# Pacing the sample's steps against the prompt's: four entries of a table

## The chip, the cores and the metric

The kernel runs on one core of a Trainium2 chip. The metric is the device time of one execution in microseconds (us). Runs before the change gave a median of 1927.56 us (three runs, 1924.34 to 1928.93).

## The reference, cut to what matters

One layer of a decoder is computed for two groups that share the weights: a prompt of 1024 tokens, and a sample of 8 sequences with one new token each and 8192 cached positions. All is float32.

```python
# prompt
q, k, v, logf, u, z = mixer_inputs(rmsnorm(xp, g_mix), w_in, b_f, g_sgu_v)
xp = xp + merge_heads(fox_prompt(q, k, v, logf), sgu_prompt(u, z, w_s, b_s), g_att_out, g_sgu_out, w_o)
xp = xp + cross_attend(rmsnorm(xp, g_cross), *memory_kv(mem_prompt, g_mem, w_ck, w_cv), w_cq, w_co)
xp = xp + conv_ffn(rmsnorm(xp, g_ffn), zeros, w_up, conv_w, conv_b, w_down)[0]
# sample: the same layers; the attention reads the paged cache through page_table
att = fox_sample(q, k, v, logf, cache_k, cache_v, cache_logf, page_table)   # 8 rows x 8192 positions x 8 heads x 64
xs = xs + merge_heads(att, sgu_sample(u, z, w_s, b_s), ...)                # w_o
xs = xs + cross_attend(rmsnorm(xs, g_cross), cache_mem_k, cache_mem_v, w_cq, w_co)
xs = xs + conv_ffn(rmsnorm(xs, g_ffn), state_conv, w_up, conv_w, conv_b, w_down)[0]
```

## The kernel before, in words

**The prompt** is one Python generator (`prompt`). Its float32 products are each made as three TensorE products of split operands (`gemm3`, L246 to L248; in the projection L410 to L412): ScalarE rounds a loaded weight tile `wr` to `wh` (L209), VectorE takes the rest `wl` (L210). The stages, by the names that the table `PACE` uses: `p1` the input projection; `att0` and `att1` the attention of each half of the tokens; then for each half `mid0`/`mid1` (output projection `w_o`, cross-attention with `w_cq` and `w_co`) and `ffn0`/`ffn1` (the MLP: 22 pairs of `w_up` tiles in four groups, each group followed by its `w_down` part). In `out_proj` the residual is added on VectorE (L932), the row factor of the norm goes through ScalarE (L948) and GpSimd (`fac`, L949) to a ScalarE scaling (L955), and `norm_T` turns the rows on TensorE (L992) and splits them on ScalarE and VectorE (L212, L213). The stretch from the last residuals of `w_co` to those splits is called the junction below; there are four of them, before `w_cq` and before `w_up` in each half.

**The sample** is a second generator. `decode` has 148 steps. A step of it loads 1 MB of keys through a GpSimd indirect DMA (L1287), multiplies them with the query on VectorE (L1293) and sums (L1297): 128 K steps, 16 for each of the 8 rows. A value step follows 18 steps later: 1 MB of values (L1346) and four column-tiled matmuls (L1352), issued for two steps at a time. Between them stand the softmax pieces of each row (L1309 to L1341). After it `sample_rest` has 87 steps: `w_o`, `w_cq`, the cross-attention's keys (`cmk`, L1516 and L1517 on VectorE, then transposes on TensorE, L1522) and values (`cmv`, L1549), `w_co` (L258), and the MLP, which reads all of `w_up` (L1591, L1595, L1610) and `w_down` (L1629, L1634) once more, 1 MB a load, and ends in two small sums (L1647) that take a PSUM bank from the ring of the prompt's products. All of the sample's large loads share four buffers of 1 MB, `kv`, and go through GpSimd's queue.

**The pace.** The prompt's generator yields after each portion of work an estimate of its TensorE time; the driver adds it up and issues one step of the sample whenever the sum reaches the entry of `PACE` for the stage. Once `decode` is through, `phase[1]` is `"rest"`, and that entry holds until the end. A flag (`held`) lets no step be issued while a junction before an MLP or a cross-attention is issued. The numbers are units of the estimate, of which the prompt has 1483 in all; they are not microseconds of the trace.

```python
        acc[0] += t
        most = int(t / PACE[phase[1] or phase[0]]) + 1
        while bgs and not held[0] and most and acc[0] >= PACE[phase[1] or phase[0]]:
            most -= 1
            acc[0] -= PACE[phase[1] or phase[0]]
            if next(bgs[0], None) is None:
                bgs.pop()
```

The tile layer then orders the issued instructions engine by engine, and hands out the buffers of a ring in the order of issue: a prompt tile that was issued behind a sample tile of the same ring gets no bank before that one has been served. On each engine instructions then run in the written order.

Of the kernel before, what the change touches and what calls it, by code (L numbers as in the profile page):

```python
# [72 lines left out]
KS = 2  # L73
BKQ = 1
LA = (2, 2)
PACE = {'p1': 7.5, 'att0': 20.0, 'mid0': 8.0, 'ffn0': 9.0, 'att1': 15.0, 'mid1': 7.5, 'ffn1': 2.5, 'rest': 3.3}


def build(nc, tc, ctx, a, phases=None):
# [1664 lines left out]
    for t in prompt():  # L1744
# [6 lines left out]
# [6 lines that stand above are left out]
# [94 lines left out]
```

## Time and profile before

| | |
|---|---|
| median of 3 runs | 1927.56 us (1924.34 to 1928.93) |
| profiled execution: its time, its span | 1927.71 us, 1926.0 us |
| granted TensorE clock, mean | 0.971 |
| TensorE matmul busy | 1821.5 us (95%) |
| TensorE weight loads busy | 1305.7 us (68%) |
| VectorE busy | 1403.7 us (73%) |
| ScalarE busy | 761.3 us (40%) |
| GpSimd busy | 470.1 us (24%) |
| DMA | 517.07 MB, mean 268 GB/s |

Busy shares are averages over stages with different limits. In this execution the projection runs to about 340 us, the two attention stages mostly lie between 340 and 520 us, the first half's middle between 520 and 740 us, the first MLP between 740 and 1160 us, the second half's middle to 1400 us, and the second MLP from there to the end. Busy TensorE time counts matmuls as the profile models them, and says where TensorE waits, not how near it is to its peak.

### The profile page before, as it was taken

How to read it: one execution, taken by the hardware profiler on the slowest of the kernel's cores; microseconds unless marked ns; L12 is line 12 of the kernel's file. 1: busy time of each engine (PE TensorE's matmuls, PEld its weight loads, DVE VectorE, ACT ScalarE, POOL GpSimd, SP SyncE). 2: the span in 40 equal slices, each digit the busy share in tenths (PEclk: the TensorE clock that was granted, in tenths of full speed). 3: DMA queues.
4: the chain of work that ended last, by engine and by line, in shares of the span. 5: the costliest groups of instructions: out<-in, count | busy, mean ns of one | idle time of the engine just before them, and what ended most of it. 6: DMA issues, size and time to landing. Idle time of an engine off the chain costs nothing.

```text
span 1926.0 us, 24250 instructions
## 1 busy us (share of the span) xinstructions
PE 1821.5 (95%) x9255; PEld 1305.7 (68%) x9255; DVE 1403.7 (73%) x1662; ACT 761.3 (40%) x1435; POOL 470.1 (24%) x429
## 2 busy tenths in 40 slices
PE   8999989788899899999999999998999999999986
PEld 5987667555676667777777776765776576876752
DVE  4887668777687776999899999878777255965412
ACT  5332366566632435323333333325344143243311
POOL 1322241222122322324123124133312201210121
PEclk9999999889999999999999999999999999999978
DMA  8876897644496865869677889877767945857785
GB/s 321 292 267 224 294 347 263 226 144 160 159 366 256 321 232 211 333 245 367 256 280 298 297 313 362 327 295 276 277 242 255 355 171 206 293 218 217 257 315 199
DMA packets 156372, 517.07 MB, mean 268 GB/s; under 512 B 20168, under 2 KB 41928, under 8 KB 123488
## 3 DMA queue, kind: packets, MB, share of 16 engines
q0 software_dynamic: 56400, 339.04, 47.0%
q1 hardware_dynamic: 92944, 163.89, 24.2%
q10 hardware_dynamic: 6912, 12.59, 1.7%
q8 instruction: 73, 1.20, 0.2%
q14 instruction: 43, 0.35, 0.1%
HBM read 493.63 MB, written 21.84 MB: 268 GB/s over the span
## 4 chain that ended last, share of the span: by engine, by line
PE 64%; DVE 6%; issue 6%; ACT 3%; POOL 1%; DMA 1%; POOLq 0%; DVEq 0%; ACTq 0%
PE ba L246 11%; PE ba L247 11%; PE ba L248 11%; PE bb L246 5%; PE dv L1352 5%; PE bb L247 5%; PE bb L248 5%; DVE kv L1293 1%; DVE s L1297 1%; PE ba L1078 1%; PE bb L772 1%; PE ba L728 1%; PE bb L756 1%; PE ba L1104 1%; DMA kv<-w_down 1%
## 5 line engine op out<-in xcount | busy, mean ns | idle before, releaser
L209 ACT ACTIVATE wh<-wr 128x1024 fp32r<-128x1024 f32 (+2 forms) x220 | 229.0, 1044 | 457.5 <-PE ba L247 145.9
L210 DVE TENSOR_TENSOR wl<-wr,wh 128x1024 fp32r<-128x1024 f32 (+2 forms) x220 | 261.7, 1201 | 114.7 <-PE ba L248 50.2
L1293 DVE TENSOR_TENSOR kv<-kv,d 128x2048 f32<-128x2048 f32 (+1 forms) x139 | 292.3, 2114 | 35.8 <-DMA kv<-cache_k,kidx 35.7
L1297 DVE TENSOR_REDUCE s<-kv 128x32 f32<-128x2048 f32 (+1 forms) x139 | 292.1, 2108 | 0.8
L1287 POOL DMA_INDIRECT kv<-cache_k,kidx x128 | 172.1, 1345 | 493.6 <-DVE s L1297 191.0
L1346 POOL DMA_INDIRECT kv<-cache_v,kidx x128 | 171.0, 1336 | 487.8 <-DVE s L1297 216.1
L246 PE MATMUL ba<-wh,u 128*128 128x512 f32 (+1 forms) x679 | 261.0, 386 | 0.1
L247 PE MATMUL ba<-wl,u 128*128 128x512 f32 (+1 forms) x679 | 258.5, 382 | 0.0
L248 PE MATMUL ba<-wh,u 128*128 128x512 f32 (+1 forms) x679 | 256.1, 381 | 0.0
L246 PE MATMUL ba<-u,wh 128*128 128x512 f32 (+2 forms) x552 | 216.5, 393 | 1.5 <-DVE u L213 1.1
L247 PE MATMUL ba<-u,wh 128*128 128x512 f32 (+2 forms) x552 | 216.3, 392 | 0.3 <-DVE u L213 0.3
L248 PE MATMUL ba<-u,wl 128*128 128x512 f32 (+2 forms) x552 | 215.1, 390 | 0.0
L246 PEld LDWEIGHTS ba<-wh,u 128*128 128x128 f32 x679 | 128.1, 189 | 36.4 <-issue 10.5
L247 PEld LDWEIGHTS ba<-wl,u 128*128 128x128 f32 x679 | 128.2, 189 | 31.6 <-issue 7.6
L248 PEld LDWEIGHTS ba<-wh,u 128*128 128x128 f32 x679 | 127.9, 188 | 31.3 <-issue 6.5
L1352 PE MATMUL dv<-kv,s 128*32 128x512 f32 x1024 | 134.0, 611 | 0.0
L246 PEld LDWEIGHTS ba<-u,wh 128*128 128x128 f32 x552 | 104.9, 190 | 36.6 <-issue 10.1
L246 PE MATMUL bb<-u,wh 128*128 128x512 f32 (+2 forms) x312 | 124.2, 398 | 1.7 <-DVE u L213 1.7
L247 PEld LDWEIGHTS ba<-u,wh 128*128 128x128 f32 x552 | 105.1, 190 | 29.4 <-issue 7.2
L247 PE MATMUL bb<-u,wh 128*128 128x512 f32 (+2 forms) x312 | 123.4, 396 | 0.0
L248 PEld LDWEIGHTS ba<-u,wl 128*128 128x128 f32 x552 | 104.9, 190 | 26.6 <-issue 4.6
L248 PE MATMUL bb<-u,wl 128*128 128x512 f32 (+2 forms) x312 | 122.4, 392 | 0.0
(404 smaller groups left out, 2969.1 us busy)
## 6 DMA issues: line engine op xcount, KB each, us to landing
wr<-w_up SPq DMA_DIRECT2D x88, 512.0 KB
kv<-w_up POOLq DMA_DIRECT2D x22, 1024.0 KB
wr<-w_down SPq DMA_DIRECT2D x40, 512.0 KB
kv<-w_down POOLq DMA_DIRECT2D x11, 1024.0 KB
wr<-w_in SPq DMA_DIRECT2D x16, 512.0 KB
wr<-w_o SPq DMA_DIRECT2D x16, 512.0 KB
wr<-w_cq SPq DMA_DIRECT2D x16, 512.0 KB
wr<-w_co SPq DMA_DIRECT2D x16, 512.0 KB
```

Source lines behind the costliest of these rows:

```text
L209: nc.scalar.activation(h, src, AF.Copy)
L210: nc.vector.tensor_tensor(l, src, h.bitcast(F32), op=ALU.subtract)
L246: mmul(out, sh, mh, start=(i == 0), stop=False)
L247: mmul(out, sh, ml, start=False, stop=False)
L248: mmul(out, sl, mh, start=False, stop=(i == n - 1))
L728: mmul(s, qab[j][:, 0, i * P : (i + 1) * P], ka[j][:, ch * n : ch * n + n], start=True, stop=False)
L756: nc.tensor.transpose(tr[:, c * P : (c + 1) * P], p_[:, kt * P : (kt + 1) * P], ident)
L1287: nc.gpsimd.indirect_dma_start(kv, None, a["cache_k"], off(kidx[:, b, ch : ch + 1]))
L1293: nc.vector.tensor_tensor(kvv[:, i : i + m, :], kvv[:, i : i + m, :], qb.unsqueeze(1).broadcast_to((P, m, 512)), op=ALU.mult)
L1297: nc.vector.tensor_reduce(s[:, ch * 4 + i : ch * 4 + i + m, :].rearrange("p k h -> p (k h)"), kvv[:, i : i + m, :].rearrange("p k (h d) -> ...
L1346: nc.gpsimd.indirect_dma_start(kv, None, a["cache_v"], off(kidx[:, b, ch : ch + 1]))
L1352: mmul(dv[32 * j : 32 * j + 32, :], s[:, ch * 4 : ch * 4 + 4, :].rearrange("p k h -> p (k h)"), kvv[:, j, :], start=(ch == 0), stop=(ch == ...
```

## The change

Four entries of the table are smaller, so a step of the sample is issued after less of the prompt's work in the projection (7.5 to 7.0), the first MLP (9.0 to 8.5), the second half's middle (7.5 to 6.8) and in everything that follows `decode` (3.3 to 2.9). No instruction is added or removed; their places change.

```diff
-PACE = {'p1': 7.5, 'att0': 20.0, 'mid0': 8.0, 'ffn0': 9.0, 'att1': 15.0, 'mid1': 7.5, 'ffn1': 2.5, 'rest': 3.3}
+PACE = {'p1': 7.0, 'att0': 20.0, 'mid0': 8.0, 'ffn0': 8.5, 'att1': 15.0, 'mid1': 6.8, 'ffn1': 2.5, 'rest': 2.9}
```

Counted in the order in which the two kernels are issued, the steps of `decode` lie like this:

| stage | p1 | att0 | att1 | mid0 | ffn0 | mid1 | ffn1 |
|---|---|---|---|---|---|---|---|
| before | 28 | 6 | 5 | 21 | 41 | 23 | 25 |
| after | 30 | 6 | 5 | 21 | 44 | 24 | 19 |

The 149th of these calls already enters `sample_rest`, whose further 87 steps follow in `ffn1` in both.

## The prediction

> **What bounds the kernel now.** I read the engines' busy time first, then their course in 40 slices, then tables of busy time by stage, then the time lines of the places that stand out. The slices show an attention part in which no engine is full, a long part in which TensorE is, and a fall at the end:
>
> ```profile
> PE 1821.5 (95%) x9255; PEld 1305.7 (68%) x9255; DVE 1403.7 (73%) x1662; ACT 761.3 (40%) x1435; POOL 470.1 (24%) x429
> PE   8999989788899899999999999998999999999986
> DVE  4887668777687776999899999878777255965412
> ```
>
> The stages (window; busy us and count of TensorE, its weight loads, VectorE, ScalarE, GpSimd; granted clock; DMA share; GB/s) are the projection without its start, the first MLP, two junctions of the second half, the start of the second MLP, the sample's cross-attention keys, and three pieces of the end:
>
> ```profile
> 60.00:340.00 280.00, 273.85 (x1507) 212.08 (x1494) 218.53 (x210) 116.46 (x205) 75.94 (x59) 0.99 0.78 279
> 790.00:1155.00 365.00, 365.00 (x1692) 269.33 (x1691) 339.15 (x315) 123.30 (x190) 103.69 (x73) 1.00 0.80 296
> 1225.00:1262.00 37.00, 33.77 (x175) 26.20 (x174) 30.30 (x33) 12.14 (x24) 6.80 (x7) 0.95 0.62 228
> 1380.00:1402.00 22.00, 17.46 (x91) 12.71 (x90) 21.20 (x16) 13.55 (x25) 10.16 (x9) 0.96 0.74 283
> 1410.00:1550.00 140.00, 140.00 (x694) 92.64 (x694) 82.66 (x107) 45.54 (x71) 28.85 (x28) 1.00 0.75 282
> 1627.00:1690.00 63.00, 63.00 (x273) 51.12 (x272) 60.70 (x58) 18.25 (x26) 13.85 (x23) 1.00 0.79 278
> 1797.00:1848.00 51.00, 51.00 (x400) 35.71 (x392) 15.23 (x22) 13.57 (x26) 9.30 (x13) 1.00 0.77 272
> 1848.00:1904.00 56.00, 41.31 (x262) 16.72 (x258) 2.12 (x5) 4.02 (x8) 11.42 (x16) 0.76 0.86 322
> 1904.00:1926.00 22.00, 12.51 (x49) 8.66 (x49) 11.19 (x22) 5.93 (x16) 3.71 (x5) 0.84 0.25 98
> ```
>
> In both MLPs TensorE is never without work, so there the time is TensorE's work, the prompt's and the sample's. The change alters no work: it can only alter the time that TensorE stands idle. So each edit is costed at the place it leaves and the place it enters, by TensorE's idle time there.
>
> **Prices.** A prompt product takes 0.23 us of TensorE, a pair of value steps 1.85 us, so 0.93 us a step. A K step takes VectorE 2.28 + 2.28 = 4.56 us (medians in the first MLP):
>
> ```profile
> 1362.34 1.85 PE dv L1352 x16
> 1364.62 0.23 PE ba L247
> L1293 DVE TENSOR_TENSOR kv<-kv,d x35: 2269/2281/2335, 796.6 to 1144.9; 128x2048 f32<-128x2048 f32 x35
> L1297 DVE TENSOR_REDUCE s<-kv x37: 2262/2277/2293, 789.1 to 1147.8; 128x32 f32<-128x2048 f32 x37
> ```
>
> **The change part by part.** The steps are unchanged in number; 2 of them move into the projection, 3 into the first MLP, 1 into the second half's middle, 6 out of the second MLP. Of those 6 calls 4 had a K step before, none has one after; the last K step is issued before the junction into the second MLP.
>
> *The last junction (1380 to 1402 us).* Here VectorE's queue holds six halves of K steps among the residuals that TensorE's transposes wait for. The time line of VectorE, and GpSimd's row factors (in brackets the idle time before one, and what ended it):
>
> ```profile
> 1379.84 2.28 DVE L1293 TENSOR_TENSOR kv<-kv,d 128x2048 f32<-128x2048 f32 x1
> 1382.15 2.29 DVE L1297 TENSOR_REDUCE s<-kv 128x32 f32<-128x2048 f32 x1
> 1384.36 0.68 DVE L932 TENSOR_TENSOR u<-ba,u 128x512 f32<-128x512 f32 x1
> 1384.95 2.28 DVE L1293 TENSOR_TENSOR kv<-kv,d 128x2048 f32<-128x2048 f32 x1
> 1387.27 2.29 DVE L1297 TENSOR_REDUCE s<-kv 128x32 f32<-128x2048 f32 x1
> 1389.47 0.68 DVE L932 TENSOR_TENSOR u<-ba,u 128x512 f32<-128x512 f32 x1
> 1393.20 2.28 DVE L1293 TENSOR_TENSOR kv<-kv,d 128x2048 f32<-128x2048 f32 x1
> ...
> 1398.27 2.27 DVE L1297 TENSOR_REDUCE s<-kv 128x32 f32<-128x2048 f32 x1
> 1381.09 1.44 POOL L949 TENSOR_TENSOR fac<-fac,mhalf 128x1 f32<-128x1 f32 x1 [10.13 <-ACT fac L948]
> 1393.86 2.04 POOL L949 TENSOR_TENSOR fac<-fac,mhalf 128x1 f32<-128x1 f32 x1 [2.81 <-ACT fac L948]
> 1400.98 0.54 POOL L949 TENSOR_TENSOR fac<-fac,mhalf 128x1 f32<-128x1 f32 x1 [5.08 <-ACT fac L948]
> ```
>
> The changed order has no K step in this stretch; in its place stand the softmax pieces of the last row, most of them a fraction of a microsecond, two of them sums of about 1.1 us. TensorE is idle for 22.0 - 17.46 = 4.5 us here. I take 4.0 of them as gained; the bounds are 0 (the softmax pieces delay as much) and 4.5.
> The factor's 1.44 and 2.04 us against 0.54 us fall where a K product is running: both end 0.4 us after that product does (1382.12 and 1395.48). The Trainium skill, "SBUF — State Buffer", section "SBUF: two separate sides", says that a VectorE instruction with two SBUF inputs and a GpSimd one that reads SBUF exclude each other through a shared port. The trace agrees with it; by that rule (2.04 - 0.54 = 1.5 us of the idle time is this lock) the gain lies at the upper bound and the sum would be 0.5 us lower.
>
> *The junction before the second half's cross-attention (1225 to 1262 us).* K halves between its last residuals and splits: 9 before, 7 after. Idle 37.0 - 33.77 = 3.2 us; 2/9 of it is 0.7 us. Bounds 0 and 3.2.
>
> *Value steps.* Six leave the second MLP, where TensorE has no idle time: 6 x 0.93 = -5.6 us. Three enter the first MLP, equally full: +2.8 us. Three enter the projection (whose end, with the start of the attention, leaves 280.0 - 273.85 = 6.2 us idle) and the second half's middle; idle time covers them, at +2.8 us if it does not, and I take +0.5. Together -2.3 us, bounds -2.8 and 0.
>
> *The projection's K steps.* Two more, 9.1 us of VectorE, which is idle for 280.0 - 218.53 = 61 us there. What can show is a load that arrives late with VectorE's queue behind it: the prompt's splits and evacuations, for whose PSUM banks TensorE waits. The waits by releaser of this window have three such, 14.3 us, the longest 4.8:
>
> ```profile
> DVE kv L1293 <- DMA kv<-cache_k,kidx: 14.3, 3, 4.8
> ```
>
> One more wait of that kind is the upper bound, 4.8; less than nothing would need a wait that goes, for which no reason is seen. TensorE lost 6.2 us in all beside these 14.3, so I take +0.5.
>
> *The first MLP's K steps.* Three more: 13.7 us of VectorE. Its idle time is 365.0 - 339.15 = 25.9 us, so I cost them at nothing; the cover is this idle time, and without it they cost 13.7 us (a rival below).
>
> *The sample's later layers.* In the order of TensorE the sample's transposes of the keys' scores (L1522) come 248 prompt products after its `w_cq` ends, where they came 284 after it: 36 x 0.23 = 8.3 us earlier. They need the last of eight sums on VectorE, which ends at 1683.71 + 2.28 = 1686.0 us:
>
> ```profile
> 1683.71 2.28 DVE L1517 TENSOR_REDUCE sS<-kv 128x8 f32<-128x2048 f32 x1
> L1522 PE MATMUL ms<-cp,sS x2: 271/272/272, 1692.6 to 1692.7; 128*32 128x128 f32 x2
> ```
>
> The margin was 1692.6 - 1686.0 = 6.6 us, and VectorE was busy for 60.70 of 63 us. In the new order more of the prompt's VectorE work stands among these sums (35 instructions, 24.9 us by their times here, for 24 with 21.0). If VectorE is late by all that, TensorE waits 8.3 + 3.9 - 6.6 = 5.6 us, and all prompt products queue behind L1522. Against it: VectorE's newest prompt work ahead of the last sum is further behind TensorE in the new order, so it starts with less to do. I take +0.5, bounds 0 and 5.6.
>
> *The tail.* One would expect most here: from 1848 to 1904 us TensorE executes nothing of the prompt, because the sample's last sums hold a place in the ring of PSUM banks and the prompt's next tile waits behind them. The denser pace moves that place, but does not free it: in the new order the same block (the last four of eleven pairs of `w_up`, all of `w_down`) stands before product 5449 of 5760 instead of 5716, and the pairs ahead of it come 22 products apart as before. So 312 products follow the block instead of 45, and the block stays as long: 56 us, of which 56.0 - 41.31 = 14.7 us are idle even by the profile's generous count. I cost this at 0. Bounds: -14.7 us, if the sample's loads get ahead; and +6.5 us, since the prompt now has loads left that can compete with the sample's: four buffers of 512 KB, 2.1 MB at the 322 GB/s of this window:
>
> ```profile
> wr<-w_up SPq DMA_DIRECT2D x88, 512.0 KB
> ```
>
> **The sum**: -4.0 - 0.7 - 2.3 + 0.5 + 0 + 0.5 + 0 = -6.0 us. The profiled execution took 1927.71 us, 0.15 above the median of the three runs, so the forecast is 1921.7 us, 0.3% below. About 0.2%, 3.9 us, is what a measurement can tell from no change.
>
> **The rivals.**
> *VectorE becomes the bound of the first MLP.* It is busy for 339.15 of 365 us there, and no row shows whether a queue that runs in order can use the last 7%. If none of its idle time can be used, the 13.7 us come on top: 1921.7 + 13.7 = 1935.4 us, slower. It decides once VectorE's work between two K steps exceeds TensorE's: 339.15 + 13.7 = 352.9 against 365 + 2.8, so 15 us of idle time have to be out of reach. For it speaks how full the queue is; against it that TensorE shows no idle time there at all. [...] Chance 0.27.
> *The cross-attention's wait.* L1522 comes too early by the full 5.6 us in place of 0.5: 1921.7 + 5.1 = 1926.8 us, no change. For it speaks a VectorE at 96%, against it the newest work behind TensorE. Chance 0.15.
> *The tail closes.* The block's idle time goes, the sample being further on when the prompt meets it: 1921.7 - 14.7 = 1907.0 us. Against it speaks the order, which has the same pairs left. Chance 0.08. That the denser pace does nothing at the end is thus my forecast itself.
>
> **How the numbers follow.** The forecast's case has 0.50. Its own range, with the junctions' and the small terms' bounds, is 1917 to 1926 us; 0.40 of it lies more than 0.2% below the median, 0.10 within it. The cross-attention's wait gives 0.10 within and 0.05 above 0.2%. So: faster 0.40 + 0.08 = 0.48; the same 0.10 + 0.10 = 0.20; slower 0.05 + 0.27 = 0.32. The range of 8 in 10 takes in the forecast, the wait, and the first MLP's rival up to 1937 us; downward it reaches to 1912 us, some way into a partly closed tail, and leaves out the rest of that.
>
> **What would show it.** Right: at the junction into the second MLP no L1293 among the residuals, `fac` at about 0.55 us, and TensorE idle for about 0.5 us. The block without prompt products lies at least 61 us earlier (267 products by 0.23 us), is about 56 us long, and full-speed products 0.23 us apart follow it for over 70 us. The first MLP is about 3 us longer, with no TensorE waits. Wrong: waits of TensorE or its weight loads for VectorE in the first MLP (the first rival); idle time ahead of L1522 (the second); a block well under 50 us (the third), or one over 62 us, which I would have mis-sized.

## The result and the profile after

The changed kernel takes 1940.41 us (median of 6 runs, 1934.43 to 1943.31), the kernel before 1926.69 us (median of 6, 1917.97 to 1932.44): the ratio is 1.0071, 95% interval 1.0049 to 1.0093. It is 0.7% slower where 0.3% faster was forecast, and lies above the whole range. The profiled execution took 1940.05 us with a span of 1938.3 us, 12.3 us more than the span before.

The busy time of the changed kernel and its course in 40 slices:

```profile
PE 1820.7 (94%) x9255; PEld 1299.1 (67%) x9255; DVE 1405.0 (72%) x1662; ACT 759.4 (39%) x1435; POOL 488.2 (25%) x429
PE   8999989778899999999999999997999998999798
DVE  4888668777687777989898988887754459553144
PEclk9999999889999999999999999998999998999899
```

TensorE does the same work in the same busy time (1820.7 us for 1821.5). The 12.3 us are idle time of TensorE: 102.5 us between its first and last matmul, where it was 88.3. The hole at the end of the slices has moved forward, from the 40th slice to the 38th; a dip in the 28th is deeper than before, and a small one in the 34th is new.

To find the place, each stretch is bounded by two of the prompt's 5760 products (single TensorE matmuls of its split operands, in their order), so that it holds the same prompt work in every kernel. Lengths in us, worked out from the TensorE rows; three experiments, told of below, stand beside the two kernels. Each column is one execution: that of the last took 1917.65 us, where the median of its kernel is 1912.9.

| prompt products | before | only "rest" denser | only the first three denser | after | after, last sums out of the ring |
|---|---|---|---|---|---|
| start to 2064 (to the first MLP) | 781.5 | 780.5 | 778.6 | 776.6 | 779.8 |
| 2064 to 3504 (first MLP) | 379.1 | 379.0 | 383.4 | 383.5 | 383.7 |
| 3504 to 3888 | 118.2 | 118.2 | 116.1 | 118.7 | 116.0 |
| 3888 to 3984 (second cross-attention) | 72.3 | 77.7 | 82.9 | 85.2 | 83.0 |
| 3984 to 4080 | 24.3 | 24.3 | 26.2 | 26.1 | 26.1 |
| 4080 to 4176 (last junction) | 33.5 | 32.4 | 29.3 | 30.6 | 30.7 |
| 4176 to 4656 | 139.5 | 139.5 | 139.9 | 139.9 | 139.9 |
| 4656 to 5040 (most of the second group's `w_up` part, its `w_down` part) | 103.4 | 103.4 | 111.9 | 111.4 | 112.8 |
| 5040 to 5715 (with the block) | 254.4 | 274.5 | 228.4 | 247.9 | 226.1 |
| 5715 to the end | 19.8 | 18.3 | 17.8 | 18.4 | 17.8 |
| span | 1926.0 | 1947.8 | 1914.5 | 1938.3 | 1915.9 |

Against before, the changed kernel loses 12.9 us in the second cross-attention, 8.0 in the stretch at 4656 and 4.4 in the first MLP, and gains 4.9 us ahead of the first MLP, 2.9 in the last junction and 6.5 in the stretch of the block. Windows of the changed kernel (busy us and count of TensorE, its weight loads, VectorE, ScalarE, GpSimd; granted clock; DMA share; GB/s) over the first MLP, the second cross-attention, the last junction, the middle of the stretch at 4656, and the block:

```profile
776.60:1160.10 383.50, 382.84 (x1766) 276.25 (x1764) 353.37 (x326) 128.94 (x197) 125.49 (x78) 1.00 0.80 296
1278.80:1364.00 85.20, 71.82 (x328) 44.83 (x327) 67.24 (x62) 34.93 (x79) 29.99 (x22) 0.92 0.84 318
1390.10:1420.70 30.60, 28.76 (x143) 22.34 (x141) 18.66 (x26) 18.21 (x33) 6.34 (x7) 0.94 0.69 254
1622.30:1643.80 21.50, 13.63 (x49) 10.53 (x49) 21.50 (x25) 4.66 (x7) 1.99 (x3) 0.76 0.67 224
1802.30:1856.90 54.60, 39.52 (x261) 14.91 (x259) 5.60 (x10) 6.94 (x13) 11.42 (x16) 0.84 0.87 339
```

The kernel before in the second cross-attention and the last junction:

```profile
1278.80:1351.10 72.30, 66.93 (x313) 42.49 (x312) 58.86 (x60) 33.90 (x78) 25.57 (x18) 1.00 0.80 305
1375.40:1408.90 33.50, 28.96 (x139) 23.30 (x138) 25.06 (x23) 17.15 (x32) 10.86 (x9) 0.90 0.74 283
```

So TensorE's idle time goes from 5.4 to 13.4 us in the cross-attention and from 4.5 to 1.8 in the junction; in the block it is 15.1 us, as before.

**The cross-attention.** What TensorE waits for there in the changed kernel (us in total, times, longest), and the piece of the chain of waits that leads to the longest of these (start, length):

```profile
PE ba L1062 <- DMA t<-o_mk: 6.7, 1, 6.7
PE ba L1096 <- ACT u L1089: 6.1, 2, 3.3
```

```profile
1299.55 0.37 SPq L223
1299.97 16.21 DMA t<-o_mk
1316.32 1.10 PE ba L1062 x4
```

The 256 KB of the prompt's memory keys take 16.2 us to land, in a stretch in which the core's DMA moves 318 GB/s, most of it the sample's gathered keys and values (GpSimd's queue moves 15.25 of the 18.52 MB from 1285 to 1345 us). Before, the same load was issued at 1298.5 us and had landed at 1305.7, 7.2 us later, and TensorE had other work until then. The waits of the kernel before, for the scaled weights of ScalarE (L1096) and for the keys of the next head:

```profile
PE ba L1096 <- ACT u L1089: 2.6, 2, 1.9
PE bb L1062 <- DMA t<-o_mk: 0.5, 1, 0.5
```

So two waits have grown: that for the keys to 6.7 us, and that for ScalarE from 2.6 to 6.1.

**The stretch at 4656.** Here TensorE has one long wait, and VectorE's queue shows why. First the wait, then TensorE around it, then VectorE during it (start, length; in brackets the idle time):

```profile
PE bb L246 <- DVE t L1178: 7.9, 1, 7.9
```

```profile
1626.28 0.40 PE L248 MATMUL ba<-wh,u 128*128 128x512 f32 x1
1634.55 0.76 PE L246 MATMUL bb<-wh,u 128*128 128x512 f32 x1 [7.87 <-DVE t L1178]
1635.11 0.63 PE L247 MATMUL bb<-wl,u 128*128 128x512 f32 x1
...
1638.95 0.61 PE L247 MATMUL ba<-wl,u 128*128 128x512 f32 x1
1639.38 0.42 PE L246 MATMUL ba<-wh,u 128*128 128x512 f32 x1
1639.63 0.39 PE L247 MATMUL ba<-wl,u 128*128 128x512 f32 x1
```

The order in VectorE's queue is seen best in the chain of waits, which runs through VectorE alone in these microseconds (the piece called issue is a weight split on VectorE, L210, 1.21 us long):

```profile
1625.22 2.27 DVE kv L1516 x2
1627.48 2.17 DVE sS L1517
1629.66 1.07 issue
1630.73 1.22 DVE kv L1516
1631.95 0.66 DVE t L1175
1632.61 1.13 DVE kv L1516
1633.74 0.66 DVE t L1176
1634.55 0.76 PE bb L246
```

VectorE is busy for all of the 21.5 us (the window above). The products and sums of the sample's cross-attention keys (L1516, L1517) stand between the convolutions of the last `w_up` tiles (L1175, L1176), and the group's `w_down` part, which begins at 1622.3 us, waits 7.9 us for a convolution to free a PSUM bank. It is not the transposes L1522, where the prediction looked for a wait: they start at 1653.7 us without one. Before, this `w_down` part began at 1615.3 us, ahead of the first key product, and VectorE had room:

```profile
1612.00:1660.00 48.00, 48.00 (x210) 35.92 (x210) 35.76 (x35) 10.85 (x14) 12.42 (x21) 1.00 0.74 267
```

### The profile page after: what moved, and what is told of

Same layout as the page of the kernel before. It is cut to its first block, busy times and chain, and to the rows that moved or that the text cites. A ratio compares the mean times of both kernels' runs of the same rounds, so it can differ in the third digit from the quotient of the medians.

```text
span 1938.3 us, 24236 instructions
## 1 busy us (share of the span) xinstructions
PE 1820.7 (94%) x9255; PEld 1299.1 (67%) x9255; DVE 1405.0 (72%) x1662; ACT 759.4 (39%) x1435; POOL 488.2 (25%) x429
## 4 chain that ended last, share of the span: by engine, by line
PE 50%; issue 11%; DVE 7%; DMA 6%; ACT 3%; POOL 3%; POOLq 0%; DVEq 0%; SPq 0%; ACTq 0%
PE ba L246 8%; PE ba L247 8%; PE ba L248 8%; PE bb L246 4%; PE bb L247 4%; PE bb L248 4%; PE dv L1352 4%; DMA kv<-cache_v,kidx 2%; POOL kv L1346 1%; DVE s L1297 1%; DVE kv L1293 1%; PE ba L1104 1%; PE bb L772 1%; DMA t<-o_mk 1%; DMA kv<-w_down 1%
## 5 line engine op out<-in xcount | busy, mean ns | idle before, releaser
L209 ACT ACTIVATE wh<-wr 128x1024 fp32r<-128x1024 f32 (+2 forms) x220 | 228.9, 1044 | 431.7 <-PE ba L247 149.5
L210 DVE TENSOR_TENSOR wl<-wr,wh 128x1024 fp32r<-128x1024 f32 (+2 forms) x220 | 262.1, 1200 | 148.5 <-PE ba L248 71.1
L1287 POOL DMA_INDIRECT kv<-cache_k,kidx x128 | 176.1, 1376 | 570.2 <-DVE s L1297 250.3
L1346 POOL DMA_INDIRECT kv<-cache_v,kidx x128 | 190.2, 1486 | 374.3 <-DVE s L1297 151.7
L246 PE MATMUL ba<-u,wh 128*128 128x512 f32 (+2 forms) x560 | 218.9, 392 | 1.1 <-DVE u L213 0.7
L247 PE MATMUL ba<-u,wh 128*128 128x512 f32 (+2 forms) x560 | 219.3, 392 | 0.1
L1352 PE MATMUL dv<-kv,s 128*32 128x512 f32 x1024 | 134.1, 609 | 0.0
L246 PE MATMUL bb<-wh,u 128*128 128x512 f32 (+1 forms) x313 | 122.1, 390 | 8.7 <-DVE t L1178 7.9
L248 PEld LDWEIGHTS ba<-u,wl 128*128 128x128 f32 x560 | 105.8, 189 | 34.3 <-issue 12.6
L246 PE MATMUL bb<-u,wh 128*128 128x512 f32 (+2 forms) x304 | 121.3, 399 | 2.2 <-DVE u L213 2.2
L247 PE MATMUL bb<-u,wh 128*128 128x512 f32 (+2 forms) x304 | 120.9, 398 | 0.0
```

The source lines that it names most:

```text
L209: nc.scalar.activation(h, src, AF.Copy)
L210: nc.vector.tensor_tensor(l, src, h.bitcast(F32), op=ALU.subtract)
L246: mmul(out, sh, mh, start=(i == 0), stop=False)
L247: mmul(out, sh, ml, start=False, stop=False)
L248: mmul(out, sl, mh, start=False, stop=(i == n - 1))
L1287: nc.gpsimd.indirect_dma_start(kv, None, a["cache_k"], off(kidx[:, b, ch : ch + 1]))
```

## The experiments

**Each half of the change.** The first kernel keeps the three paces of `decode` and makes only `rest` denser, the second does the reverse.

```diff
-'p1': 7.5, 'ffn0': 9.0, 'mid1': 7.5, 'rest': 3.3
+'p1': 7.5, 'ffn0': 9.0, 'mid1': 7.5, 'rest': 2.9     # only rest
+'p1': 7.0, 'ffn0': 8.5, 'mid1': 6.8, 'rest': 3.3     # only the first three
```

> Only the sample's later layers are denser (3.3 to 2.9); the decode's steps stand as in the kernel before. In the order of TensorE everything up to the sample's key transposes (L1522, before product 5217 of the prompt) is as before, so the profile should match the kernel before up to about 1690 us. Theory A (the loss of the changed kernel comes from where the decode's steps, and with them the sample's cross-attention, now fall): no wait of 8 us in the second half's cross-attention and none among the sample's keys; the time differs from before only by the tail, within 4 us of it. Rival B (the denser later layers are the loss, through VectorE among the sample's keys): 8 to 9 us slower than before. Rival C (the first MLP's VectorE): no change.

> The three decode entries are changed, the later layers keep 3.3. The order is that of the changed kernel up to L1522 (before product 4981 in both). Theory A: both waits are there as in the changed kernel, 13 us idle against 5 in the second half's cross-attention and about 9 us among the sample's keys, 3 us less at the junction into the second MLP; the time is 10 to 15 us over before. Rival B: the wait among the keys is gone, at most 5 us over before.

Measured: only `rest` 1948.42 us against 1925.55, ratio 1.0109 (1.0083 to 1.0134); only the first three 1918.90 us, ratio 0.9961 (0.9944 to 0.9979). One half of the change makes the kernel faster and the other, by more, slower: -6.6 and +22.9 us, together +16.3, where both at once measure +13.7. Both expectations missed the time, since both took the tail for unchanged: within 4 us of before was expected of the first, and 10 to 15 us over before of the second, whose two waits did come (10.7 and 9.9 us of idle time). By the table, the first three bring the loss of 19 us in the two stretches with them, but also a gain of 26.0 us between 5040 and 5715, and `rest` costs 20.1 us in that same stretch. In the order of instructions, `rest` alone changes nothing on any engine before the sample's own MLP. The block without prompt products, in the kernel with only `rest`; the whole tail from 5424 to 5715 in that with only the first three:

```profile
1788.00:1887.00 99.00, 77.28 (x547) 37.19 (x545) 6.61 (x13) 10.07 (x18) 21.25 (x30) 0.69 0.87 324
```

```profile
1789.90:1896.70 106.80, 101.89 (x595) 67.83 (x592) 40.45 (x64) 32.06 (x60) 13.40 (x19) 1.00 0.64 229
```

Between two neighbouring prompt products the longest gap is 57.9 us before, 98.7 with only `rest`, 17.7 with only the first three, 54.6 with all four. The place of the sample's last sums in the ring of PSUM banks is set by the pace at which the steps are issued: 87 steps by 0.4 puts it 35 units of the estimate earlier when `rest` is denser. But how far the sample is at that place isn't set by this pace: its pairs of `w_up` come 22 products apart from product 5314 on with both values of `rest` (before, with the old paces of `decode`, from 5581 on), and what is left of them at the place makes the block. With only `rest` the place is at 5544 and all eleven pairs fall into the block, with only the first three it is at 5616 and none does.

**The first three paces apart.**

```diff
-'p1': 7.5, 'ffn0': 9.0, 'mid1': 7.5, 'rest': 3.3
+'p1': 7.5, 'ffn0': 9.0, 'mid1': 6.8, 'rest': 3.3     # only mid1
+'p1': 7.0, 'ffn0': 8.5, 'mid1': 7.5, 'rest': 3.3     # only p1 and ffn0
```

> Only the second half's middle is denser (7.5 to 6.8): ten value steps instead of eight among the prompt's second cross-attention (products 3888 to 3984), as in the changed kernel, while the steps before it stand as before. Theory A1 (the density in the middle makes the wait for the prompt's own key loads there): TensorE idle about 13 us between these products, 8 more than before. Theory A2 (it is only where the steps happen to fall, moved by the two earlier entries): idle about 5 us as before. Sample's keys: the transposes come before product 5048, among the start of a group of the MLP, so a wait there of 0 to 9 us is open.

> The projection and the first MLP are denser, the second half's middle and the later layers are as before: nine value steps among the prompt's second cross-attention. A1: idle there 5 to 7 us, close to before. A2: about 13 us. Sample's keys: the transposes come before product 4979, nearly where the changed kernel has them (4981), so theory A expects its wait of about 9 us. Rival C (the first MLP's VectorE is the bound): the first MLP is 10 us or more longer than before, against 4 in the changed kernel.

Measured: only `mid1` 1923.94 us, ratio 0.9988 (0.9971 to 1.0005); only `p1` and `ffn0` 1923.89, ratio 0.9997 (0.9978 to 1.0015). Neither can be told from no change. The idle time of the second cross-attention is 5.7 us with the denser pace in that very stage, and 15.1 us with it only in the projection and the first MLP: it is not the number of steps there that costs, but which step arrives there. The 15.1 us are other waits than those of the changed kernel: 6.3 us for a load of the sample's own values (L1352), which TensorE has in its order ahead of the prompt's work, and 8.1 for ScalarE, none for `o_mk`. The idle time at 4656 comes with each of them (10.8 and 8.2 us), but not as one wait for the convolution either: with `mid1` alone it is 4.1 us for a weight split on VectorE (L210) and 6.7 for a residual of the `w_down` part (L1207), with `p1` and `ffn0` alone 2.1 us for the convolution and 5.2 for a split on ScalarE (L209). The tail is free of idle time with `p1` and `ffn0` alone, and has 5.2 us with `mid1` alone.

**The ring itself.** If the place in the ring is the cause, the loss has to go when the last sums take their PSUM tiles from the sample's own pools, all paces kept as changed. The same edit in the kernel before tells whether the tie alone was the loss.

```diff
-            ps = BK()
+            ps = (DV, MS)[n]()
```

> The changed kernel with all four new paces; the sample's two last sums (L1646 to L1647) take their PSUM tiles from the sample's own pools instead of the prompt's ring of accumulators. The steps' paces are not touched. In the order of the instructions on TensorE this spreads the 176 products of w_up over prompt products 5314 to 5534 and puts the last w_down product at 5672, where the changed kernel has 64 of w_up and all 44 of w_down bunched at 5448. Theory 'the ring's place': the loss of the changed kernel is the tail, where the prompt's tiles wait behind a tile that the sample needs last. With the tie gone the block of 23 us goes with its idle and its low clock: 5424 to 5715 in 103 to 107 us instead of 126, the run at 1915 to 1921 us, ratio to before 0.994 to 0.998. Theory 'density': the loss is the denser steps themselves (the cross-attention wait of +8, the keys' wait of +9, and loads that crowd the DMA engines in the last layers); then it stays within 5 us of the changed kernel, 1935 to 1942.

> The kernel before, all paces old; only the sample's two last sums take their PSUM tiles from the sample's own pools. In the order on TensorE, w_up then runs from 5581 to the end of the prompt's 5760 products, and w_down, the last sums and the sample's norm come after all of them. Theory 'the ring's place': the block at 5715 goes, but what the sample still has to do comes after the prompt's last product: 5424 to 5715 takes 103 to 110 us instead of 154, of which some 35 to 45 us come back behind 5760 as a tail of the sample alone. Between 1915 (the 45 prompt products and the prompt's norm now run beside the loads) and 1930. If the tie alone were what the decode's paces bring, this kernel would come to e2's 1919 or below; if denser decode is needed to bring the sample forward, it stays within 8 us of before.

Measured: the changed kernel without the tie 1912.9 us against 1925.13, ratio 0.9936 (0.9913 to 0.9959); the kernel before without it 1925.53, ratio 1.0005 (0.9988 to 1.0023). The changed kernel without the tie over the 56 us in which the block lay, then the kernel before without it from its last prompt products on:

```profile
1802.50:1858.80 56.30, 56.30 (x370) 40.37 (x369) 26.27 (x40) 19.71 (x36) 9.06 (x13) 1.00 0.78 285
```

```profile
1863.70:1923.70 60.00, 31.64 (x182) 10.36 (x180) 10.95 (x24) 8.49 (x21) 12.21 (x17) 0.79 0.67 266
```

Prompt and sample now run beside each other at full clock; behind product 5040 no gap between two prompt products is over 4 us, and 5040 to 5715 falls from 247.9 to 226.1 us. That is 21.8 of the 22.4 us between the two spans: the theory of the ring's place holds, that of the denser loads falls. The time lies 2 us below the 1915 to 1921 that were expected. In the kernel before, the same edit moves the work only: 57.6 us less up to product 5715, 56.8 more after it, where the sample alone still loads `w_up` and `w_down`. So it takes both, a sample that is far enough on and a prompt that doesn't wait for it. The expectation for the second kernel had the part that comes back at 35 to 45 us, which was too little.

With the tie gone, the two paces of `rest` give the same order on all five engines. Whatever `rest` does in this kernel, it does through the tie. This version, the fastest of all that were run, is faster than both kernels; against the one with only the first three paces (0.9961) the intervals overlap, so the two can't be told apart.

**The keys' wait.** The sample's steps are spread, up to the keys' products, in the kernel without the tie.

```diff
-        phase[1] = "rest"
+        phase[1] = "head"        # 6.0; "rest" again behind the keys
```

> As the first kernel of this call (all four new paces, last sums out of the ring), and the sample's last layers run from their start up to the cross-attention's keys at a pace of 6.0 in place of 2.9, so that the products for the keys move from 4536...5230 to 4536...5344 and stand apart from one another; w_up then ends at 5642 and 16 products of w_down and the last sums stand at the end of the prompt. Theory 'VectorE's queue': the 9 us of idle between products 4656 and 5040 come of key steps that are bunched at the end of the up part, where VectorE is full; spread out, they fall to 0 to 4, and against the first kernel of this call the run is 2 to 8 us faster unless the tail behind product 5760 takes it back (up to 10 us). Rival 'the place': the wait is one of the place in the down part's start, not of the bunching: then the idle stays at 8 to 10 and this kernel is 0 to 10 us slower than the first of this call, by its tail.

Measured: 1923.0 us, ratio 0.9989 (0.9973 to 1.0005), 10.1 us more than without the spreading. The idle time between 4656 and 5040 stays at 10.3 us, in four pieces of 2.1 to 2.8 us in place of one, the last of them ahead of L1522: bunching is not the cause. That the place is, as the rival has it, fits, but is not shown by this. The tail behind 5715 grows by 16.5 us (34.3 for 17.8) while 5040 to 5715 shrinks by 10.1.

**Only `mid1`, without the tie.**

```diff
-'p1': 7.0, 'ffn0': 8.5, 'mid1': 6.8, 'rest': 2.9
+'p1': 7.5, 'ffn0': 9.0, 'mid1': 6.8, 'rest': 3.3
```

> Only the second half's middle at its new pace (6.8); projection, first MLP and the sample's later layers at the old ones; last sums out of the ring. The cross-attention of the second half, which lost 8 us with the new paces of projection and first MLP and nothing with this pace alone, keeps its old time (idle 5 to 6 us between 3888 and 3984); the tail is free (last sums at 5745 of 5760). Theory 'the ring's place' with the waits as separate prices: 1915 to 1921 us, some 3 to 8 us below the same paces with the tie (1923.9), and within 4 us of the first kernel of this call: what it saves in the cross-attention it lacks in the first cross-attention (-2.7) and the junctions. Theory 'density': no difference from the same paces with the tie, 1923 to 1925.

Measured: 1922.58 us, ratio 0.9988 (0.9973 to 1.0003). The cross-attention keeps its 6.8 us of idle time, as expected, and 5040 to 5715 falls from 236.4 to 224.7 us; but the last sums stand at product 5745 of 5760, and from 5715 to the end it takes 28.6 us for 18.1. Expected were 1915 to 1921 us: this tail was missing from the expectation. So the tie's removal pays only where the sample ends early enough: 66 products before the prompt's end it did, 15 before it didn't.

**The steps in the cross-attention, and the first MLP.** Both kernels are without the tie. The decode's steps are moved out of the second cross-attention and paid for by denser paces ahead of it; then, in a second kernel, the first stages are made denser still and nothing is moved.

```diff
-'p1': 7.0, 'ffn0': 8.5, 'mid1': 6.8
+'p1': 6.6, 'ffn0': 7.8, 'mid1': 6.0, 'cross1': 12.0     # a stage of its own for the second cross(xt, sq)
+'p1': 6.6, 'ffn0': 8.0, 'mid1': 6.8                     # the second kernel
```

> The four new paces with the last sums out of the ring, and the steps of the decode moved out of the second half's cross-attention: a pace of 12.0 there in place of 6.8, paid for by 6.6 in the projection, 7.8 in the first MLP and 6.0 ahead of the cross-attention, so that the decode ends at the same product and everything from the sample's later layers on stands at the same products (5314 to 5534, 5587, 5694). Between products 3888 and 3984 stand 4 value steps in place of 10; before product 3504 there are 88 in place of 82. Two questions, each read in its own stretch. The cross-attention: theory 'the gathered loads of the decode's own steps hold up the prompt's o_mk loads there' says idle from 3888 to 3984 falls from 11.0 to 2 to 5 us; the rival 'the cross-attention's own chain (ScalarE, then TensorE) waits in any case' says 8 to 11. The first MLP: the rival of the prediction, VectorE as its bound, has its test here: 6 more K steps are 27 us of VectorE work, more than the 12 us that are left of its 25.9 us of idle time, so by that rival the MLP grows by 15 us or more with idle TensorE time (383.7/0.9 to about 400/10 or more); if TensorE's idle time stays under 2 us, VectorE is still no bound there and the growth is that of the value steps, 5 to 6 us. In all: 1905 to 1912 us if the cross-attention frees up and the MLP holds; 1918 to 1930 if the MLP binds.

> The four new paces with the last sums out of the ring, and projection and first MLP denser still (6.6 and 8.0 in place of 7.0 and 8.5): 4 more steps before product 3504, and everything behind moves 40 to 60 products forward (the scores' transposes of the sample's cross-attention from 4980 to 4920, w_up from 5268, last sums at 5659). The keys' wait: theory 'the place' says that it comes when the sample's eight key steps are in VectorE's queue while the down part of the second MLP's first group begins (product 4896): here they still are, so 8 to 10 us of idle time between 4656 and 5040 stay; the rival 'the up part's end alone' (VectorE full only in the last third of the up part) says that it falls under 5. The cross-attention: by 'alignment of loads' any value from 5 to 15 us. In all 1908 to 1918 us, no better than the first of the free kernels by more than 4 us; if density in itself were still worth something once the ring's tie is gone, it would come below 1908.

Measured: 1925.25 us, ratio 1.0001 (0.9986 to 1.0015), and 1934.39 us, ratio 1.0050 (1.0031 to 1.0068). The first kernel's windows over the first MLP and the second cross-attention:

```profile
795.20:1186.30 391.10, 388.04 (x1795) 276.67 (x1793) 365.54 (x329) 128.43 (x196) 144.83 (x86) 1.00 0.84 311
1314.80:1378.40 63.60, 60.99 (x277) 42.39 (x276) 41.86 (x44) 32.66 (x77) 10.48 (x10) 1.00 0.67 244
```

With 4 value steps in place of 10 the cross-attention has 2.6 us of idle time for 11.0, no wait for `o_mk`, and takes 63.6 us for 83.0, at 244 GB/s for 329: the wait there is made by the sample's own steps. In the second kernel the ten value steps are back, and the idle time is 6.8 us, all of it for ScalarE. The first MLP has 3.1 us of idle time, more than the 2 under which VectorE was to count as no bound, but it grows by 7.4 us, not by 15 or more, though VectorE's work rises by 12 us and four more value steps run there: VectorE isn't its bound. Yet in all the kernel loses 10.2 us of span against the one without the tie and with the changed paces, and misses the 1905 to 1912 us that were expected: 15.4 us go ahead of the first MLP and 12.5 between 3504 and 3888, where the steps went. The second kernel loses nearly the same there (15.1 and 13.7), so at these paces the projection, the attention and the second half's merge have no room left for steps. Ahead of the first MLP the largest new wait is again for a load of the prompt's own, the queries of its attention (L677, `t<-q_d`: 7.1 and 9.5 us, no such wait in the kernel that both are compared with). The second kernel's keys' wait is 4.4 us, under the 5 that the rival set. There 6 of the 8 key sums are done by product 4896, where the `w_down` part begins; where 4 are done it is 8 to 10 us, where none is, though the key products have begun, 10 to 11, and it is gone where they begin well behind it (before, from product 4941 on, 0.0). What sets its size is open.

## Why the prediction was wrong

Its direction failed at two waits that it had priced at nearly nothing, and it took a tail that hadn't changed for one that nothing had acted on. It also counted steps by the stage that issues them; in the traces they execute elsewhere. By its own terms, against the kernel before:

- *The last junction*, -4.0: measured -2.9 us, idle time 4.5 to 1.8. The mechanism was right. The K products have left it, and three of the four row factors take about 0.55 us (the last of them, at 1413.62, isn't shown); one is held up by a VectorE weight split instead. GpSimd's rows, then that VectorE row:

```profile
1397.74 0.57 POOL L949 TENSOR_TENSOR fac<-fac,mhalf 128x1 f32<-128x1 f32 x1
1402.19 0.54 POOL L949 TENSOR_TENSOR fac<-fac,mhalf 128x1 f32<-128x1 f32 x1 [3.88 <-ACT fac L948]
1408.18 1.51 POOL L949 TENSOR_TENSOR fac<-fac,mhalf 128x1 f32<-128x1 f32 x1 [5.44 <-ACT fac L948]
```

```profile
1408.06 1.23 DVE L210 TENSOR_TENSOR wl<-wr,wh 128x1024 fp32r<-128x1024 f32 x1
```

- *The junction before the second cross-attention*, -0.7: the stretch 3504 to 3888, in which it lies, took 118.7 us for 118.2. Nothing was gained: from 1225 to 1262 us VectorE has eight K halves in both traces, not 9 and 7, and TensorE is idle for 3.0 us, where it was 3.2.
- *Value steps*, -2.3: the six did leave the second MLP (18 for 24 from 4176 to 4656), and the sample's later layers moved into their room (139.9 us for 139.5). What was gained by it stands at the end: between 5040 and 5715 the sample has 36 matmul records fewer (620 for 656), and the stretch is 6.5 us shorter with the same 15.1 us of idle time. What failed is the other side. Idle time was to cover the steps that enter the second half's middle, for +0.5 us; where two of them arrived, in the second cross-attention, it grew instead (below).
- *The projection*, +0.5: the first 1152 products take 2.9 us longer (266.2 for 263.3). Up to the first MLP the kernel is nevertheless 4.9 us shorter, since the first half's cross-attention (products 1728 to 1920) gains 5.1 (100.9 to 95.8), as it does within 1 us in every kernel that has the same paces up to there. The prediction didn't see this one.
- *The first MLP*, 0 beside the value steps' +2.8: measured +4.4 us, of which 0.7 is idle time. It isn't the three value steps: 37 of them run in that stretch in both kernels (38.4 us in both). One more closing sum of a row (L1377, three for two) takes 2.6 us with the wait behind it, and 84 of the prompt's products, next to the sample's matmuls, are followed only 0.33 us later, for 60 before: 2.3 us. The rival with VectorE as its bound falls, in the changed kernel, where only one more K product runs in that stretch (39 for 38), and in the kernel with 42 of them.
- *The second cross-attention*: no term but the value steps' cover by idle time, measured +12.9 us, 8.0 of it idle time. This is the first step that failed. The prediction counted one more step into `mid1` (in the trace 10 value steps and 10 K products run there, for 8 and 8) and looked at the value steps' TensorE time, not at the megabyte that each one loads beside the prompt's own loads. The stretch is not very steady either: it took 72.3, 77.7 and 74.0 us in three kernels whose order is the same up to there. The loss of 12.9 stands above this spread, and with 10 to 11 us it is there again in all three other kernels with the first three paces (the two of the table, and the one with the keys spread).
- *The sample's later layers*, +0.5 (bounds 0 to 5.6): measured +8.0 us with 8.9 of idle time, above the upper bound. This is the second step that failed. The prediction followed TensorE's own instruction (L1522) and asked whether its input would be late; what was late was the prompt's convolution behind the same VectorE work. It read its term from the order with all four paces; the wait comes with the first three alone (9.9 us) and is 0.0 with `rest` alone.
- *The tail*, 0: the block is 54.6 us long for 57.9, idle for 15.1 us in both, and 73 us of prompt products follow it. It begins 46 us earlier (1802.3 for 1848.4), not 61, since the stretches ahead of it are longer. As a comparison of the two kernels the term was right, by luck: two changes that cancel made it. Its reason, "the denser pace moves that place, but does not free it", was true of one half of the change only. The decode's paces alone all but free the block (-26.0 us from 5040 to 5715), and the pace of `rest` brings it back (+19.5, from 228.4 to 247.9). Costed apart, the two edits would have shown a sum of large terms with opposite signs instead of a zero.
- The rival "the tail closes" came about in the kernels where `rest` is left alone or the tie is gone. The price set on it, 14.7 us of idle time, was too small: with the paces of `decode` changed, some 20 to 22 us hung on the block (247.9 us from 5040 to 5715, against 228.4 with the old `rest` and 226.1 without the tie), for inside it fewer matmuls run at a lower granted clock (261 records in 54.60 us, 39.52 of them busy, at 0.84, against 370 in 56.30 at 1.00 without the tie).

What it comes to: +20.9 us in two stretches, with the waits that the first three paces bring, less 8.6 us net elsewhere, is the 12.3 us of the spans. The first three paces alone paid for those waits with the tail; `rest` took that back.

## What to carry to other kernels

Where a background stream shares a ring of buffers with the main one, the order of issue fixes which main tile waits for which background tile, and a denser pace makes that tie earlier without bringing the background's work forward: cost such a pace by how far the stream really is at the tie, and take its last tiles out of the ring. Cost the edits of one change one by one even where they seem to cancel, because a zero can be two large terms. For a step that moves, look beyond the instruction that consumes it: at the transfers that land late beside its loads, and at the other work that stands behind it in the queue of its busiest engine.

## What the runs showed of the hardware

- A wait of TensorE costs more than its length. Behind the 7.9 us wait at 1626 the prompt's products start 0.43 us apart (1635.11, 1635.54, ...) and come back to 0.23 us only at 1639.4, 4.8 us later; the granted clock of that window is 0.76. In those 4.8 us ten products cost some 2 us more than at full rate. The Trainium skill, "TensorE: Matmul & The Clock Gate", Part 1, gives half rate after an idle window of about 3.4 us and full rate again after about as much sustained work. The trace agrees with the halving, and its 4.8 us are somewhat longer.
- A 256 KB load that was needed at once took 16.2 us to land beside gathered loads, in a stretch with 318 GB/s for the core; the same load took 7.2 us before, in a stretch with 305 GB/s, and 8.3 in the one with fewer of the sample's steps (244 GB/s), where TensorE didn't wait for it at all. The average rate alone doesn't tell such a load's time.
- The row factor on GpSimd took 1.51 us beside VectorE's weight split with two inputs (L210) and 0.54 us with VectorE idle; before, it was K products that held it up. It ends 0.4 us after the VectorE instruction in all three cases (1409.69 here, after 1409.29).
